# Moving matmul operands to other places modulo 512 bytes in a hybrid RWKV-7 / attention / gated-MLP layer

## The chip, the cores and the metric

The kernel runs on one core of one Trainium2 chip. The metric is the device time of one execution in microseconds (us), as a median over runs.

## The reference

One layer of a streaming encoder, 256 tokens by 2048 features, all in float32:

```python
u   = rms_norm(h) * g;  z = u @ w_in                 # 2048 -> 3360 + 1088 + 4096 columns
A   = rwkv7_mixer(z[:, :3360])                       # 16 heads x 64, a delta-rule scan
B   = mla_mixer(z[:, 3360:4448])                     # 8 heads, low-rank q and kv
g_rw, g_mla = split(sigmoid(z[:, 4448:]))
mix = (g_rw * (A @ w_branch_rw) + g_mla * (B @ w_branch_mla)) @ w_out
h  += rms_norm(mix)
up  = causal_dwconv(rms_norm(h) @ w_up)              # 2048 -> 2 x 5632, width 3
gate, val = split(up)
h  += rms_norm((gelu(gate) * val) @ w_down)          # 5632 -> 2048
h  += rms_norm(sigmoid(h @ w_ple_gate) * (p @ w_ple))
```

## The kernel before

Every large product is done in fp32r with both operands split into two parts, `hi` (the value rounded to fp32r) and `lo` (what is left), and three products of parts are summed: hi·hi, hi·lo and lo·hi. Weights come in chunks of 512 KB (128 partitions x 1024 numbers) on SyncE's DMA queue into one of three `raw` buffers; `wchunk` (L147 to L175) has ScalarE copy each half to a `hi` buffer (L166) and VectorE subtract it to a `lo` buffer (L167), five buffers of 128x512 of each kind.

Four helpers issue the matmuls. In the first two the weights are the stationary operand (128 columns, loaded anew for each matmul) and the activations move.

- `fm3` (L197): three matmuls of 256 columns for each weight block, hi·hi (L201), hi·lo (L202), lo·hi (L203). It serves the input projection (moving tile `uT`), the two branch projections (`ymla`, `yrw`) and the low-rank up-projections (`latm`).
- `fm` (L183): two matmuls for each weight block, one of 512 columns with the hi weights over the activation's hi and lo part in one go (L192, or L190 for the last block of a sum) and one of 256 columns with the lo weights over the hi part (L193, or L189). It serves the MLP's up-projection alone (tile `u2`, which the trace shows as `u`). The two halves of the PSUM bank are added later by `conv_sum`.
- `tm` (L208): here the activations are stationary (128 tokens) and the weights move, 512 columns: L214, L216, L218. It serves the products with `w_out` (stationary tile `mixs`), `w_down` (`fsplit`), `w_ple_gate` (`h2T`), and the value projection (`latm` stationary, moving `hi` and `lo`).
- small fp32 matmuls of the attention and of the RWKV scan are woven between the `fm3` matmuls.

An activation tile such as `uT` or `u2` holds 16 blocks of 512 numbers a partition, each block the 256 hi parts and then the 256 lo parts of 128 features. `fsplit` holds the two parts of one block of `f`, the MLP's middle activations, and stands in the pool `fs` at the right end of the memory.

Where a tile stands in a partition's memory is decided when the program is built. The buffers of the weights, `hi` and `lo`, all stand at 64 bytes modulo 512, and so does every 128-column block of them, which is 512 bytes long. The places of the other operand, in bytes modulo 512, in the built program:

| tile | role | before | after |
|---|---|---|---|
| `uT`, `ymla`, `yrw` | moving, 256 columns | 64 | 96 |
| `latm` | moving, 256 columns | 96 | 96 |
| `u2`, hi and lo in one | moving, 512 columns | 64 | lo part 64; hi part 96 (blocks 0 to 7), 64 (blocks 8 to 15) |
| `u2`, hi | moving, 256 columns | 64 | 96 (blocks 0 to 7), 64 (blocks 8 to 15) |
| `fsplit` | stationary | 480 | 64 |
| `mixs`, `h2T` | stationary | 64 | 64 |
| `latm` | stationary | 96 | 96 |

Of the kernel before, what the change touches and what calls it, by code (L numbers as in the profile page):

```python
# [7 lines left out]
F32 = mybir.dt.float32  # L8
F32R = mybir.dt.float32r
I32 = mybir.dt.int32  # L10
AF = mybir.ActivationFunctionType
ALU = mybir.AluOpType
# [3 lines left out]
P = 128  # L16
T = 256
D = 2048
KB = D // P
C = 64  # L20
NCH = T // C
NPAIR = 8
NFF = 44
WC = 1024
NH = 8
# [101 lines left out]
def hybrid_block(tc, A):  # L127
    nc = tc.nc
    es = ExitStack()
    mm = nc.tensor.matmul  # L130
    act = nc.scalar.activation
    tt = nc.vector.tensor_tensor
    ts = nc.vector.tensor_scalar
    stt = nc.vector.scalar_tensor_tensor
# [43 lines left out]
    def split(hi, lo, src):  # L178
        act(hi, src, AF.Copy)  # L179
        tt(out=lo, in0=src, in1=hi.bitcast(F32), op=ALU.subtract)  # L180


    def fm(ps, hi, lo, cols, mov, first, last):  # L183
        n = len(mov)
        for c, col in enumerate(cols):
            for i in range(n):
                f, l = first and i == 0, last and i == n - 1
                if l:
                    mm(ps[:, c, 0:T], lo(i, col, P), mov[i][:, 0:T], start=False, stop=False)  # L189
                    mm(ps[:, c, :], hi(i, col, P), mov[i], start=f, stop=True)  # L190
                else:
                    mm(ps[:, c, :], hi(i, col, P), mov[i], start=f, stop=False)  # L192
                    mm(ps[:, c, 0:T], lo(i, col, P), mov[i][:, 0:T], start=False, stop=False)  # L193


    def fm3(ps, hi, lo, cols, mov, first, last):
# [52 lines left out]
    def to_fm(ptile, dst, rows, gain, kbs):  # L249
        for k in range(kbs[0], kbs[1], 2):  # L250
            ps = ptile("tr")
            for kb in (k, k + 1):
                o = ps[:, (kb - k) * T:(kb - k) * T + T]
                for t in range(2):
                    nc.tensor.transpose(o[:, t * P:t * P + P], rows[:, t, kb * P:kb * P + P], ident)  # L255
                if gain is not None:
                    g = V(gain, kb)
                    a = act(dst[:, kb, 0:T], o, AF.Copy, scale=g)
                    v = stt(out=dst[:, kb, T:2 * T], in0=o, scalar=g, in1=dst[:, kb, 0:T].bitcast(F32),
                            op0=ALU.mult, op1=ALU.subtract)  # L260
            if gain is None:
                o = ps[:].rearrange("p (k t) -> p k t", k=2)
                a = act(dst[:, k:k + 2, 0:T], o, AF.Copy)
                v = tt(out=dst[:, k:k + 2, T:2 * T], in0=o, in1=dst[:, k:k + 2, 0:T].bitcast(F32), op=ALU.subtract)
        return a, v


# [1 line left out]
    esp = ExitStack()  # L269
    big = es.enter_context(tc.tile_pool(name="big", bufs=1))  # L270

    def act_tile(nm):
        return big.tile([P, KB, 2 * T], F32R, name=nm, tag="act")

    def row_tile(nm, s, shape=None, dt=F32):
        return big.tile(shape or [P, 2, D], dt, name=nm, tag=f"row{s}")

    uT = act_tile("uT")
    psd = esp.enter_context(tc.tile_pool(name="psd", bufs=4, space=PSUM))
    pss = esp.enter_context(tc.tile_pool(name="pss", bufs=2, space=PSUM))  # L280
    nsm = [0]
# [8 lines left out]
    xT = row_tile("xT", 0, [P, KB, T])  # L290
# [3 lines left out]

    def x_split(kb):
        g = V("g_pre", kb)
        act(uT[:, kb, 0:T], xT[:, kb, :], AF.Copy, scale=g)
        stt(out=uT[:, kb, T:2 * T], in0=xT[:, kb, :], scalar=g, in1=uT[:, kb, 0:T].bitcast(F32),
            op0=ALU.mult, op1=ALU.subtract)

    def x_part(q):
# [10 lines left out]
        nc.sync.dma_start(x, xr[:, t, c])  # L312
        act(x, x, AF.Square, accum_out=st[:, i:i + 1])

    umov = [uT[:, kb, :] for kb in range(KB)]
    es_z = ExitStack()
    zp = es_z.enter_context(tc.tile_pool(name="zp", bufs=2, side="right"))
    es_e = ExitStack()
# [112 lines left out]
    h, l = [], []  # L431
    for c in range(2):
        x_split(2 * c)
        hi = wp.tile([P, 512], F32R, name="hi", bufs=5)
        lo = wp.tile([P, 512], F32R, name="lo", bufs=5)
# [81 lines left out]
    ps = run(dense(umov, [A["w_in1"][q] for q in range(2)], 8, cols=(0,)))  # L517
# [7 lines left out]
    ps = run(win_duo(0))  # L525
# [24 lines left out]
    p = slice(64, 96)  # L550
# [7 lines left out]
    for i in range(2):  # L558
        p = slice(64 * i, 64 * i + 64)
# [11 lines left out]
    def u_part(q):  # L571

        for kb in range(4 * q, 4 * q + 4):
            stt(out=xT[:, kb, :], in0=xT[:, kb, :], scalar=V("g_pre", kb), in1=rsb[:], op0=ALU.mult, op1=ALU.mult)
        for kb in range(4 * q, 4 * q + 4, 2):
            split(uT[:, kb:kb + 2, 0:T], uT[:, kb:kb + 2, T:2 * T], xT[:, kb:kb + 2, :])

    qp = []
    for j in range(2):
        o = run(up2(A["w_q"][4 + j], cq))  # L580
# [20 lines left out]
    SC = float(192.0 ** -0.5)  # L601

    mix = row_tile("mix", 0, [P, KB, T])
    ymla = row_tile("ymla", 1, [P, NH, 2 * T], F32R)

    def attention(h, q, k):
        pr = []
# [64 lines left out]
        evac(mix[:, 2 * j:2 * j + 2, :], pb[:], scale=0.5)  # L672


    yrw = row_tile("yrw", 1, [P, NPAIR, 2 * T], F32R)
    es_e.close()
    es_e = ExitStack()
    ep = es_e.enter_context(tc.tile_pool(name="ep", bufs=1))
# [473 lines left out]
    xr2 = A["x"].rearrange("(t p) d -> p t d", p=P)  # L1152
    late_x = [load(h[:, t, c:c + 1024], xr2[:, t, c:c + 1024]) for t in range(2) for c in range(0, D, 1024)]
    mg = row_tile("mg", 1)
    u2 = act_tile("u2")
    with tc.tile_pool(name="gb", bufs=1) as gb, tc.tile_pool(name="pso", bufs=1, space=PSUM, reuse_waits="tile") as pso:
        gbc, gl = gain_bc(gb, A["g_pm"])
        tm_all(pso, A["w_out"], lambda kb: mixs[:, kb, :], post(gb, mg, gbc, 8), side=SIDE0 + gl + late_x)
# [6 lines left out]
    fp = es_f.enter_context(tc.tile_pool(name="fp", bufs=1))  # L1165
    f = fp.tile([P, NFF, T], F32, name="f")
    es_g = ExitStack()
    fsp = es_g.enter_context(tc.tile_pool(name="fs", bufs=4, side="right"))
    gb = es_g.enter_context(tc.tile_pool(name="gb2", bufs=1, side="right"))
    with tc.tile_pool(name="fw", bufs=2) as fw, tc.tile_pool(name="psu", bufs=3, space=PSUM, reuse_waits="tile") as psu:  # L1170
        u2m = [u2[:, kb, :] for kb in range(KB)]
        zc = [fp.tile([P, 2, T + 2], F32, name=f"zc{i}") for i in range(2)]
        for z in zc:
            nc.gpsimd.memset(z[:, :, 0:2], 0.0)

        def conv_sum(j, ps):
            z = zc[j % 2]
            y = fw.tile([P, 2, T], F32, name="cy")
            with tc.high_priority():
                act(y[:], ps[:, :, 0:T], AF.Copy)  # L1180
                tt(out=z[:, :, 2:T + 2], in0=ps[:, :, T:2 * T], in1=y[:], op=ALU.add)

        def conv(j):
            z = zc[j % 2]
            y = fw.tile([P, 2, T], F32, name="cy")
            tt(out=z[:, :, 2:T + 2], in0=z[:, :, 2:T + 2], in1=u2s[:].unsqueeze(1).to_broadcast([P, 2, T]), op=ALU.mult)  # L1186
            for c in range(2):
                m = j + NFF * c
                act(y[:, c, :], z[:, c, 2:T + 2], AF.Identity, bias=V("cb", m), scale=V("cw2", m))  # L1189
                stt(out=y[:, c, :], in0=z[:, c, 1:T + 1], scalar=V("cw1", m), in1=y[:, c, :], op0=ALU.mult, op1=ALU.add)  # L1190
                stt(out=y[:, c, :], in0=z[:, c, 0:T], scalar=V("cw0", m), in1=y[:, c, :], op0=ALU.mult, op1=ALU.add)  # L1191
            act(y[:, 0, :], y[:, 0, :], AF.Gelu_apprx_tanh)
            tt(out=f[:, j, :], in0=y[:, 0, :], in1=y[:, 1, :], op=ALU.mult)


        pu = {}
        for n, (j, q) in enumerate([(j, q) for q in range(4) for j in range(3)] + [(j, q) for j in range(3, NFF) for q in range(4)]):
            if q == 0:
                pu[j] = psu.tile([P, 2, 512], F32, name="d")
            ps = pu[j]  # L1200
            with queued(rows[n] if n < 2 else None):
                hi, lo = wchunk(A["w_up"][j, q], 4)
            fm(ps, hi, lo, [0, P], u2m[4 * q:4 * q + 4], q == 0, q == 3)
            if j < 2 and q == 3:
                conv_sum(j, ps)
            if (j, q) == (0, 3):
                with queued(rows[2]):
                    for t in range(2):
                        for g in range(4):
                            junk = gb.tile([P, 512], F32, name="junk", bufs=2)  # L1210
                            act(junk[:], h[:, t, g * 512:g * 512 + 512], AF.Square, accum_out=col4(18)[:, t, g:g + 1])
                r = st[:, 26:28]
                rstd4(r, 18)
            if (j, q) == (3, 0):

                rbr = fp.tile([P, 2, P], F32, name="rbr")
                for t in range(2):
                    act(rbr[:, t, :], r[:, t:t + 1].to_broadcast([P, P]), AF.Copy)
                prb = trp.tile([P, 512], F32, name="tr")
                for t in range(2):  # L1220
                    nc.tensor.transpose(prb[:, t * P:t * P + P], rbr[:, t, :], ident)
                u2s = fp.tile([P, T], F32, name="u2s")
                act(u2s[:], prb[:, 0:T], AF.Copy)
                conv(0)
                conv(1)
                conv_sum(2, pu[2])
                conv(2)
            if j > 2 and q == 3:
                conv_sum(j, ps)
                conv(j)  # L1230
# [4 lines left out]
    with tc.tile_pool(name="psw", bufs=1, space=PSUM, reuse_waits="tile") as psw:  # L1235
# [34 lines left out]
        def finish(t):  # L1270
# [3 lines left out]
            for a, n, q in ((0, 1024, nc.sync), (1024, 640, nc.scalar), (1664, 384, nc.sync)):  # L1274
# [6 lines left out]
        lp = es_f.enter_context(tc.tile_pool(name="late", bufs=1, reuse_waits="tile"))  # L1281
        late = lp.tile([P, 10, 2, 512], F32R, name="late")
        eg = lp.tile([P, 512], F32, name="eg")
        tm_all(psw, A["w_pg"], lambda kb: h2[:, kb, :], gated, 10, lambda i: (late[:, i, 0, :], late[:, i, 1, :]),
               after=rows)
    es_f.close()
    es_g.close()
# [100 lines left out]
```

## Time and profile before

| | |
|---|---|
| median of 3 runs | 1617.18 us (1614.29 to 1618.39) |
| the profiled execution | 1614.37 us, span 1612.6 us |
| PE busy | 1586.2 us, 98% of the span, 10624 matmuls |
| VectorE, ScalarE busy | 1191.5 us (74%), 968.6 us (60%) |
| DMA | 285.59 MB, 177 GB/s in the mean |
| granted TensorE clock | 1.00 of full speed (2.4 GHz) in all but the last stretch |

The span is the profiled execution from its first to its last instruction. Matmuls overlap in the pipeline, so the length of one (283 ns for 256 columns) is not what it costs: what counts is the distance from its start to the start of the next one. The stages in order of time: the input projection with attention and RWKV scan woven in (to 615 us), the RWKV branch (615 to 661), `w_out` (662 to 749), the MLP's up-projection (757 to 1257), `w_down` (1257 to 1503), the gate of the layer's embedding (1510 to 1600).

### The profile page before, as it was taken

To read this page: it belongs to the slowest core of one execution; us is meant where nothing else is said; L and a number is where in the kernel's file an instruction comes from. 1 tells how busy PE (TensorE), PEld (TensorE's weight loads), DVE (VectorE), ACT (ScalarE), POOL (GpSimd) and SP (SyncE) were. 2 spreads that over 40 slices of the span, in tenths; PEclk is the share of its full clock that TensorE was granted. 3 is DMA by queue.
4 is the path that set the end of the run, shared out by engine and by line. 5 is a ranking of instruction groups with operands and counts; after the bars stand their busy time and mean duration, and the time that the engine had idled before them with its cause. 6 is when DMAs were issued, how large, how long until landed. Compare 5 with 4: busy or idle time off the path is not lost.

```text
span 1612.6 us, 29281 instructions
## 1 busy us (share of the span) xinstructions
PE 1586.2 (98%) x10624; PEld 1420.6 (88%) x10624; DVE 1191.5 (74%) x2666; ACT 968.6 (60%) x2030; POOL 29.7 (2%) x78
## 2 busy tenths in 40 slices
PE   8999999999999999999999999999999999999997
PEld 8989999999999999887888888888888888888885
DVE  6796797878989566557787777777777655777866
ACT  6676656566565655456765555655555555666653
POOL 0000100000000001100000000000000000000000
PEclk9999999999999999999999999999999999999999
DMA  8654554444545455776566666666666666666564
GB/s 291 189 156 144 158 160 129 131 146 119 158 124 157 126 186 185 264 222 172 179 186 187 189 186 184 187 188 186 185 187 189 183 187 192 192 188 186 168 197 142
DMA packets 80048, 285.59 MB, mean 177 GB/s; under 512 B 8992, under 2 KB 10144, under 8 KB 79904
## 3 DMA queue, kind: packets, MB, share of 16 engines
q1 hardware_dynamic: 77616, 280.19, 57.3%
q10 hardware_dynamic: 2288, 3.55, 0.7%
q8 instruction: 83, 1.36, 0.3%
q14 instruction: 61, 0.50, 0.1%
HBM read 281.60 MB, written 2.10 MB: 176 GB/s over the span
## 4 chain that ended last, share of the span: by engine, by line
PE 57%; DVE 1%; ACT 0%; issue 0%; DVEq 0%; ACTq 0%
PE d L192 19%; PE d L193 10%; PE o L214 6%; PE o L216 6%; PE o L218 6%; PE e L216 2%; PE e L214 2%; PE e L218 2%; PE d L190 1%; PE d L189 1%; PE tr L255 0%; DVE h L1276 0%; DVE lo L167 0%; DVE h L1131 0%; ACT junk L1262 0%
## 5 line engine op out<-in xcount | busy, mean ns | idle before, releaser
L167 DVE TENSOR_TENSOR lo<-raw,hi 128x512 fp32r<-128x512 f32 x1012 | 685.9, 689 | 336.9 <-ACT hi L166 329.2
L166 ACT CAST hi<-raw 128x512 fp32r<-128x512 f32 x1012 | 612.6, 617 | 480.8 <-PE d L192 182.7
L192 PE MATMUL d<-u,hi 128*128 128x512 f32 x1320 | 470.8, 399 | 0.0
L193 PE MATMUL d<-u,lo 128*128 128x256 f32 x1320 | 371.3, 281 | 0.0
L201 PE MATMUL d<-uT,hi 128*128 128x256 f32 x1072 | 311.9, 291 | 5.1 <-ACT hi L179 5.1
L203 PE MATMUL d<-uT,lo 128*128 128x256 f32 x1072 | 305.5, 285 | 2.4 <-DVE lo L167 2.4
L202 PE MATMUL d<-uT,hi 128*128 128x256 f32 x1072 | 304.5, 284 | 0.0
L192 PEld LDWEIGHTS d<-u,hi 128*128 128x128 f32 x1320 | 248.1, 188 | 56.1
L193 PEld LDWEIGHTS d<-u,lo 128*128 128x128 f32 x1320 | 249.4, 189 | 4.3
L201 PEld LDWEIGHTS d<-uT,hi 128*128 128x128 f32 x1072 | 206.4, 193 | 6.9 <-ACT hi L179 5.1
L203 PEld LDWEIGHTS d<-uT,lo 128*128 128x128 f32 x1072 | 206.2, 192 | 3.4 <-DVE lo L167 2.9
L202 PEld LDWEIGHTS d<-uT,hi 128*128 128x128 f32 x1072 | 206.6, 193 | 0.1
L214 PE MATMUL o<-hi,fsplit 128*128 128x512 f32 x264 | 90.2, 396 | 0.0
L216 PE MATMUL o<-lo,fsplit 128*128 128x512 f32 x264 | 90.1, 395 | 0.0
L218 PE MATMUL o<-hi,fsplit 128*128 128x512 f32 x264 | 89.9, 394 | 0.0
L214 PEld LDWEIGHTS o<-hi,fsplit 128*128 128x128 f32 x264 | 49.6, 188 | 12.4
L216 PEld LDWEIGHTS o<-lo,fsplit 128*128 128x128 f32 x264 | 49.6, 188 | 12.0
L218 PEld LDWEIGHTS o<-hi,fsplit 128*128 128x128 f32 x264 | 49.6, 188 | 11.6
L180 DVE TENSOR_TENSOR fsplit<-f,fsplit 128x256 fp32r<-128x256 f32 x132 | 54.8, 419 | 0.0
L179 ACT ACTIVATE fsplit<-f 128x256 fp32r<-128x256 f32 x132 | 54.4, 413 | 0.7 <-ACT fsplit L179 0.5
L1189 ACT ACTIVATE cy<-zc,vec 128x256 f32<-128x256 f32 x88 | 52.7, 601 | 2.7 <-DVE zc L1186 2.6
L1191 DVE SCALAR_TENSOR_TENSOR cy<-zc,vec,cy 128x256 f32<-128x256 f32 x88 | 42.4, 482 | 1.5
(393 smaller groups left out, 2378.9 us busy)
## 6 DMA issues: line engine op xcount, KB each, us to landing
raw<-in_w_up SPq DMA_DIRECT2D x176, 512.0 KB, 3.6
raw<-in_w_in SPq DMA_DIRECT2D x133, 512.0 KB, 3.6
raw<-in_w_down SPq DMA_DIRECT2D x88, 512.0 KB, 4.3
raw<-in_w_out SPq DMA_DIRECT2D x32, 512.0 KB, 4.4
raw<-in_w_pg SPq DMA_DIRECT2D x32, 512.0 KB, 3.7
raw<-in_w_bm SPq DMA_DIRECT2D x16, 512.0 KB, 3.6
raw<-in_w_br SPq DMA_DIRECT2D x16, 512.0 KB, 4.2
raw<-in_w_kv SPq DMA_DIRECT2D x8, 512.0 KB, 3.6
```

Of the source, the lines that this page charges most:

```text
L166: nc.scalar.copy(hi[:], raw[:, c:c + 512])
L167: tt(out=lo[:], in0=raw[:, c:c + 512], in1=hi[:].bitcast(F32), op=ALU.subtract)
L179: act(hi, src, AF.Copy)
L180: tt(out=lo, in0=src, in1=hi.bitcast(F32), op=ALU.subtract)
L192: mm(ps[:, c, :], hi(i, col, P), mov[i], start=f, stop=False)
L193: mm(ps[:, c, 0:T], lo(i, col, P), mov[i][:, 0:T], start=False, stop=False)
L201: mm(ps[:, c, :], hi(i, col, P), mov[i][:, 0:T], start=f, stop=False)
L202: mm(ps[:, c, :], hi(i, col, P), mov[i][:, T:2 * T], start=False, stop=False)
L203: mm(ps[:, c, :], lo(i, col, P), mov[i][:, 0:T], start=False, stop=l)
L214: mm(b[:], h, hi(i, g * 512, 512), start=f, stop=False)
L216: mm(b[:], h, lo(i, g * 512, 512), start=False, stop=False)
L218: mm(b[:], x, hi(i, g * 512, 512), start=False, stop=l)
```

## The change

All tiles keep their sizes in numbers that are used, and every engine issues the same instructions in the same order with the same waits on the same semaphores; only addresses, and the access patterns of `fm`, differ.

- `uT` starts 8 numbers (32 bytes) into its allocation; `ymla` and `yrw` likewise.
- `u2` is laid out apart: first the 16 lo parts, then the 16 hi parts, the first eight of these 32 bytes further on, the last eight 512 bytes further on.
- `fm`'s 512-column matmul reads the lo part and then the hi part, through an access pattern of two runs of 256; so the lo-weight product is added to the second half of the PSUM bank and no longer to the first.
- A tile `pad` of 104 numbers (416 bytes) at the right end moves the pool `fs`, so that `fsplit` comes to 64 modulo 512.
- The allocations of `uT`/`u2`/`h2T` and of `ymla`/`yrw` grow by 128 numbers (512 bytes), which moves all that stands behind them by a multiple of 512 bytes.

```diff
@@ fm
+            o = ps[:, c, :].rearrange("p (a t) -> p a t", a=2)
             for i in range(n):
                 f, l = first and i == 0, last and i == n - 1
+                h, _, both = mov[i]
                 if l:
-                    mm(ps[:, c, 0:T], lo(i, col, P), mov[i][:, 0:T], start=False, stop=False)
-                    mm(ps[:, c, :], hi(i, col, P), mov[i], start=f, stop=True)
+                    mm(ps[:, c, T:2 * T], lo(i, col, P), h, start=False, stop=False)
+                    mm(o, hi(i, col, P), both, start=f, stop=True)
                 else:
-                    mm(ps[:, c, :], hi(i, col, P), mov[i], start=f, stop=False)
-                    mm(ps[:, c, 0:T], lo(i, col, P), mov[i][:, 0:T], start=False, stop=False)
+                    mm(o, hi(i, col, P), both, start=f, stop=False)
+                    mm(ps[:, c, T:2 * T], lo(i, col, P), h, start=False, stop=False)
@@ tiles
-    def act_tile(nm):
-        return big.tile([P, KB, 2 * T], F32R, name=nm, tag="act")
+    def act_tile(nm, o=lambda k: 0, apart=False):
+        t = big.tile([P, KB * 2 * T + 128], F32R, name=nm, tag="act")
+        if not apart:
+            return [(t[:, x:x + T], t[:, x + T:x + 2 * T], t[:, x:x + 2 * T]) for x in (o(k) + 2 * T * k for k in range(KB))]
+        return [(t[:, x:x + T], t[:, T * k:T * k + T],
+                 bass.AP(t[:].tensor, t[:, T * k:T * k + T].offset, [t[:].ap[0], [x - T * k, 2], [1, T]]))
+                for k, x in ((k, o(k) + KB * T + T * k) for k in range(KB))]
...
+    def y_tile(nm):
+        return row_tile(nm, 1, [P, 16 * T + 128], F32R)[:, 8:8 + 16 * T].rearrange("p (b t) -> p b t", b=8)
+
-    uT = act_tile("uT")
+    uT = act_tile("uT", lambda k: 8)
-    ymla = row_tile("ymla", 1, [P, NH, 2 * T], F32R)
+    ymla = y_tile("ymla")
-    yrw = row_tile("yrw", 1, [P, NPAIR, 2 * T], F32R)
+    yrw = y_tile("yrw")
-    u2 = act_tile("u2")
+    u2 = act_tile("u2", lambda k: 8 if k < 8 else 128, True)
@@ the pools of the MLP
     es_g = ExitStack()
+    es_g.enter_context(tc.tile_pool(name="pad", bufs=1, side="right")).tile([P, 104], F32, name="pad")
     fsp = es_g.enter_context(tc.tile_pool(name="fs", bufs=4, side="right"))
```

## Rows read from the trace of the kernel before

**Rows 1.** The page: span, busy time of each engine.

```profile
span 1612.6 us, 29281 instructions
PE 1586.2 (98%) x10624; PEld 1420.6 (88%) x10624; DVE 1191.5 (74%) x2666; ACT 968.6 (60%) x2030; POOL 29.7 (2%) x78
```

**Rows 2.** Busy time by stretch: densest for VectorE, and up-projection; clock, DMA, GB/s last.

```profile
360.00:460.00 100.00, 97.64 (x967) 95.29 (x966) 87.09 (x274) 62.73 (x165) 3.87 (x14) 1.00 0.45 136
860.00:1240.00 380.00, 380.00 (x2153) 329.59 (x2152) 286.88 (x505) 221.76 (x404) 0.00 (x0) 1.00 0.62 186
```

**Rows 3.** Longest waits of ScalarE and PE: total us, times, longest.

```profile
ACT hi L166 <- PE d L192: 182.7, 165, 1.5
...
PE d L201 <- ACT hi L179: 5.1, 1, 5.1
```

**Rows 4.** Matmuls by tile: ns least, median, most; first and last start in us.

```profile
L201 PE MATMUL d<-uT,hi x1072: 276/283/582, 5.1 to 614.5; 128*128 128x256 f32 x179
...
L201 PE MATMUL d<-yrw,hi x128: 283/283/284, 614.8 to 660.5; 128*128 128x256 f32 x128
...
L214 PE MATMUL o<-hi,fsplit x264: 394/394/400, 1257.4 to 1503.1; 128*128 128x512 f32 x132
...
L214 PE MATMUL e<-hi,fsplit x88: 392/394/395, 1380.6 to 1441.5; 128*128 128x512 f32 x88
...
L192 PE MATMUL d<-u,hi x1320: 390/398/482, 756.9 to 1256.6; 128*128 128x512 f32 x189
...
L190 PE MATMUL d<-u,hi x88: 395/400/400, 786.4 to 1257.1; 128*128 128x512 f32 x88
```

**Rows 5.** Timeline of PE in the input projection: start, length, instruction.

```profile
560.93 0.36 PE L201 MATMUL d<-uT,hi 128*128 128x256 f32 x1
561.13 0.28 PE L202 MATMUL d<-uT,hi 128*128 128x256 f32 x1
...
590.10 0.28 PE L201 MATMUL d<-uT,hi 128*128 128x256 f32 x1
...
592.98 0.28 PE L201 MATMUL d<-uT,hi 128*128 128x256 f32 x1
```

**Rows 6.** Timeline of PE in the RWKV branch projection.

```profile
619.85 0.28 PE L201 MATMUL d<-yrw,hi 128*128 128x256 f32 x1
...
622.73 0.28 PE L201 MATMUL d<-yrw,hi 128*128 128x256 f32 x1
```

**Rows 7.** Timeline of PE in the low-rank up-projections.

```profile
126.11 0.28 PE L201 MATMUL d<-latm,hi 128*128 128x256 f32 x1
...
128.56 0.28 PE L201 MATMUL d<-latm,hi 128*128 128x256 f32 x1
```

**Rows 8.** Timeline of PE in the product with `w_out`, stationary `mixs`.

```profile
679.68 0.62 PE L214 MATMUL o<-hi,mixs 128*128 128x512 f32 x2
...
683.76 0.62 PE L214 MATMUL o<-hi,mixs 128*128 128x512 f32 x2
```

**Rows 9.** Timeline of PE in the product with `w_down`, stationary `fsplit`.

```profile
1300.30 0.63 PE L218 MATMUL o<-hi,fsplit 128*128 128x512 f32 x2
...
1303.10 0.63 PE L218 MATMUL o<-hi,fsplit 128*128 128x512 f32 x2
```

**Rows 10.** Timeline of PE in the value projection, stationary `latm`.

```profile
94.13 0.40 PE L214 MATMUL dv<-hi,latm 128*128 128x512 f32 x1
...
96.93 0.40 PE L214 MATMUL dv<-hi,latm 128*128 128x512 f32 x1
```

**Rows 11.** Timeline of PE in the MLP's up-projection.

```profile
1000.13 0.40 PE L192 MATMUL d<-u,hi 128*128 128x512 f32 x1
1000.37 0.28 PE L193 MATMUL d<-u,lo 128*128 128x256 f32 x1
1000.49 0.40 PE L192 MATMUL d<-u,hi 128*128 128x512 f32 x1
...
1001.19 0.40 PE L192 MATMUL d<-u,hi 128*128 128x512 f32 x1
```

More of the change, by code (lines that the diff above doesn't have):

```diff
@@ L257, in to_fm @@
                     g = V(gain, kb)
-                    a = act(dst[:, kb, 0:T], o, AF.Copy, scale=g)
-                    v = stt(out=dst[:, kb, T:2 * T], in0=o, scalar=g, in1=dst[:, kb, 0:T].bitcast(F32),
+                    a = act(dst[kb][0], o, AF.Copy, scale=g)
+                    v = stt(out=dst[kb][1], in0=o, scalar=g, in1=dst[kb][0].bitcast(F32),
                             op0=ALU.mult, op1=ALU.subtract)
@@ L262, in to_fm @@
                 o = ps[:].rearrange("p (k t) -> p k t", k=2)
-                a = act(dst[:, k:k + 2, 0:T], o, AF.Copy)
-                v = tt(out=dst[:, k:k + 2, T:2 * T], in0=o, in1=dst[:, k:k + 2, 0:T].bitcast(F32), op=ALU.subtract)
+                hi, lo = (two(dst[k][x], dst[k + 1][x]) for x in range(2))
+                a = act(hi, o, AF.Copy)
+                v = tt(out=lo, in0=o, in1=hi.bitcast(F32), op=ALU.subtract)
         return a, v
@@ L270, in hybrid_block, with two @@
     big = es.enter_context(tc.tile_pool(name="big", bufs=1))
-    def act_tile(nm):
-        return big.tile([P, KB, 2 * T], F32R, name=nm, tag="act")
+    def act_tile(nm, o=lambda k: 0, apart=False):
[5 more added lines that the diff above has]
+                for k, x in ((k, o(k) + KB * T + T * k) for k in range(KB))]
+    def two(a, b):
+        return bass.AP(a.tensor, a.offset, [a.ap[0], [b.offset - a.offset, 2], a.ap[1]])
     def row_tile(nm, s, shape=None, dt=F32):
         return big.tile(shape or [P, 2, D], dt, name=nm, tag=f"row{s}")
-    uT = act_tile("uT")
+    def y_tile(nm):
+        return row_tile(nm, 1, [P, 16 * T + 128], F32R)[:, 8:8 + 16 * T].rearrange("p (b t) -> p b t", b=8)
+    uT = act_tile("uT", lambda k: 8)
     psd = esp.enter_context(tc.tile_pool(name="psd", bufs=4, space=PSUM))
@@ L296, in x_split @@
         g = V("g_pre", kb)
-        act(uT[:, kb, 0:T], xT[:, kb, :], AF.Copy, scale=g)
-        stt(out=uT[:, kb, T:2 * T], in0=xT[:, kb, :], scalar=g, in1=uT[:, kb, 0:T].bitcast(F32),
+        act(uT[kb][0], xT[:, kb, :], AF.Copy, scale=g)
+        stt(out=uT[kb][1], in0=xT[:, kb, :], scalar=g, in1=uT[kb][0].bitcast(F32),
             op0=ALU.mult, op1=ALU.subtract)
@@ L313, in stat_part @@
         act(x, x, AF.Square, accum_out=st[:, i:i + 1])
-    umov = [uT[:, kb, :] for kb in range(KB)]
+    umov = [b[2] for b in uT]
     es_z = ExitStack()
@@ L575, in u_part @@
         for kb in range(4 * q, 4 * q + 4, 2):
-            split(uT[:, kb:kb + 2, 0:T], uT[:, kb:kb + 2, T:2 * T], xT[:, kb:kb + 2, :])
+            split(*(two(uT[kb][x], uT[kb + 1][x]) for x in range(2)), xT[:, kb:kb + 2, :])
     qp = []
@@ L1170, in hybrid_block @@
     with tc.tile_pool(name="fw", bufs=2) as fw, tc.tile_pool(name="psu", bufs=3, space=PSUM, reuse_waits="tile") as psu:
-        u2m = [u2[:, kb, :] for kb in range(KB)]
+        u2m = u2
         zc = [fp.tile([P, 2, T + 2], F32, name=f"zc{i}") for i in range(2)]
@@ L1283, in hybrid_block @@
         eg = lp.tile([P, 512], F32, name="eg")
-        tm_all(psw, A["w_pg"], lambda kb: h2[:, kb, :], gated, 10, lambda i: (late[:, i, 0, :], late[:, i, 1, :]),
+        tm_all(psw, A["w_pg"], lambda kb: h2[kb][2], gated, 10, lambda i: (late[:, i, 0, :], late[:, i, 1, :]),
                after=rows)
```

## The prediction, on record before the changed kernel ran

> **What bounds the kernel now.** I first read the page: PE is busy for 1586.2 of 1612.6 us, VectorE for 74% and ScalarE for 60% [rows 1]. An average could hide a stage with another limit, so I next read stretches. In the up-projection PE is busy for all of 380 us; in the stretch where VectorE is densest, 360 to 460 us, VectorE stands at 87.09 of 100 us and PE still at 97.64 [rows 2]. The waits say who sets the pace: ScalarE's longest wait is that for the up-projection's matmuls to give a `hi` buffer back, 182.7 us in 165 waits, while PE's longest single wait is one of 5.1 us at the start [rows 3]. So the weights are made ahead of need, and what PE saves per matmul shortens the kernel, as long as it saves a few per cent.
>
> PE's busy share says nothing of how fast it goes. For that I read the timeline and took distances from start to start, because matmuls overlap. The same shape has two prices:
>
> - 256 columns moving, place 64, weights at 64: with `uT` 24 matmuls take 592.98 − 590.10 = 2.88 us, 120.0 ns each [rows 5]; with `yrw` 24 take 622.73 − 619.85 = 2.88 us, the same [rows 6].
> - 256 columns moving, place 96, weights at 64: with `latm` 21 matmuls of the same helper take 128.56 − 126.11 = 2.45 us, 116.7 ns each [rows 7].
> - 512 columns moving at 64, stationary at 64: with `mixs` 18 matmuls take 683.76 − 679.68 = 4.08 us, 226.7 ns each [rows 8].
> - 512 columns moving at 64, stationary elsewhere: with `fsplit` (480) 12 take 1303.10 − 1300.30 = 2.80 us [rows 9], with `latm` (96) 12 take 96.93 − 94.13 = 2.80 us [rows 10]; 233.3 ns each.
>
> The helper, the columns, the instruction mix and the clock (1.00, its 2.4 GHz level [rows 2]) are the same within each pair; the place modulo 512 bytes is what differs. A weight block is read while the matmul before it streams, so two reads of the same memory run side by side, and I take it that they delay each other by their relative place. Equal places are the better ones for 512 columns and the worse ones for 256.
>
> The Trainium skill speaks against this. "TensorE: Matmul & The Clock Gate", Part 2, "Step-by-step: what each phase is for", says that PE has two independent read ports and that "Loading the next tile's weights doesn't steal SBUF read bandwidth from the running matmul". By that rule no place should cost anything and the sum below would be 0. The trace does not agree: 116.7 against 120.0 and 226.7 against 233.3 ns at one clock.
>
> **The change part by part.** No instruction, wait or order changes, so every term is a count of matmuls times a difference of distances. VectorE and ScalarE write as many numbers to the new places as before, and I cost that at nothing; what covers it is that they wait for PE [rows 3].
>
> *`uT` to place 96.* 3 × 1072 = 3216 matmuls [rows 4] go from the price of rows 5 to that of rows 7: 3.33 ns each, 10.7 us if all gain. Those next to one of the scan's small matmuls stand at other distances (561.13 − 560.93 = 0.20 us [rows 5]) that need not shrink; I take six in seven, 9.2 us. Bounds: 0 and 10.7.
>
> *`ymla` and `yrw` to place 96.* Each 3 × 128 = 384 matmuls (the count is shown for `yrw` [rows 4]). `yrw` stands alone on PE: 384 × 3.33 ns = 1.3 us. `ymla` is woven like `uT`: 1.1 us. Together 2.4 us.
>
> *`fsplit` to place 64.* 3 × (264 + 88) = 1056 matmuls [rows 4] go from the price of rows 9 to that of rows 8, 6.67 ns each: 7.0 us. Nothing else is woven in here. This is the safest term.
>
> *`u2` apart, half of it 32 bytes off.* 1320 + 88 = 1408 pairs of a 512- and a 256-column matmul [rows 4]. Three pairs take 1001.19 − 1000.13 = 1.06 us, 353.3 ns a pair [rows 11]. No row has a moving operand of two runs with two places, so I bound it. The best that nearby rows allow is 226.7 + 116.7 = 343.4 ns [rows 7, 8]: 9.9 ns less a pair, 14 us for all. The worst is the longest distances seen in this stage on every pair, 0.24 + 0.12 us [rows 11]: 6.7 ns more, 9.4 us lost. The value I take: in blocks 0 to 7 (704 pairs) the 256-column matmul is that of rows 7, hi part at 96 and weights at 64, and gains 3.33 ns, 2.3 us; the 512-column one starts on the lo part at 64 as before, and the weights read beside it are 128 columns alone, so its second half matters little: 0. In blocks 8 to 15 all places modulo 512 are as before: 0.
>
> *What is given back.* Where VectorE is at 87% [rows 2], PE's next dense stretch will now and then reach a scan step or a weight half that isn't ready. I take 1 us. What would be late next there is VectorE's `lo` and the scan's results; over the whole weave that cover gone would cost at most the `uT` and `ymla` terms, 10.3 us.
>
> Sum: 9.2 + 2.4 + 7.0 + 2.3 − 1.0 = 19.9 us. The profiled execution took 1614.37 us, so 1594.5 us; it lies 2.8 us under the median of the runs shown, 1617.18, which by the same sum goes to 1597.3. I forecast 1595.
>
> **The rivals.**
>
> *The up-projection gains in full.* If the distances there come from the same clash as elsewhere, and breaking the row of equal places frees both matmuls of a pair, all 1408 pairs reach 343.4 ns: 14 in place of 2.3 us, 1583 us. For it: a pair costs 353.3 ns, 10 more than the two best prices added. Against it: half of the blocks keep their places.
>
> *The up-projection loses.* The 512-column matmul reads two runs, of which the second stands elsewhere, and settles at the long distances of rows 11: 9.4 us lost in place of 2.3 gained, 1607 us. For it: 512 columns like equal places best [rows 8 to 10], and in blocks 0 to 7 half of the columns leave theirs.
>
> *Nothing changes.* Place is not the cause, or the scan's chain sets the weave and takes the gain back. For it: the skill's rule above, by which it would be 1614 to 1617 us. Against it: five tiles in five stages fall into the two prices by place alone, and PE hardly waits [rows 3].
>
> *Slower.* The pattern of two runs costs the 512-column matmul a restart between the runs. No row shows such a restart; the nearest is the distance after a foreign matmul, 0.20 against 0.12 us [rows 5], so between 0 and 80 ns each. It decides at (18.6 gained elsewhere, less the 1.0 given back, + 4.9) / 1408 = 16 ns: above that the kernel is slower by over 0.3%; at 80 ns it would lose 113 us and end at 1709. Against it: the prices that place makes in these rows are 3 to 7 ns a matmul, and a restart of 16 ns or more would be of another kind; but it is the step of which the trace shows least.
>
> **How the numbers follow.** My forecast (1590 to 1600 us) has 0.50; the up-projection in full (1580 to 1590) 0.22; the up-projection losing (1600 to 1608) 0.13; nothing changes 0.08; slower 0.07. About 0.3%, 4.9 us, is what a measurement of this kernel can tell from no change. Faster by more: the first three and a part of the fourth's upper edge, 0.86. Within: 0.07. Slower: 0.07. The range that leaves out nothing changed and slower, and a little of the outer ends of the second and third, is 1581 to 1607; it holds the bounds of `u2` on both sides (1583 and 1607).
>
> **What would show it.** In the trace after: 24 `uT` matmuls in 2.80 us where there were 2.88; `yrw` the same; 12 `fsplit` matmuls in 2.72 in place of 2.80 us; three `u2` pairs of blocks 0 to 7 in 1.05 us and of blocks 8 to 15 in 1.06; the up-projection's length, 757 to 1257 us before, shorter by 2 to 3 us and `w_down`'s by 7; ScalarE still waiting for PE. I am wrong if `uT` or `fsplit` keep their distances, if the 512-column distances of `u2` leave 0.23 to 0.24, or if PE's waits in the weave grow by more than some us.

## The result, and the profile after

The changed kernel takes 1601.12 us in the median of 4 runs (1598.50 to 1601.52), the kernel before, run beside it, 1617.79 us. The ratio is 0.9897 with a 95% interval of 0.9883 to 0.9911: 16.7 us less, where the forecast of 1595 us meant 22. The profiled execution took 1598.50 us against 1614.37, 15.9 us less, where its sum said 19.9.

The page after: span, PE's busy time, and ScalarE's copies with what ended the idle time before them.

```profile
span 1596.7 us, 29281 instructions
PE 1567.3 (98%) x10624; PEld 1409.5 (88%) x10624; DVE 1191.9 (75%) x2666; ACT 968.7 (61%) x2030; POOL 29.7 (2%) x78
...
L166 ACT CAST hi<-raw 128x512 fp32r<-128x512 f32 x1012 | 612.5, 617 | 464.6 <-PE d L194 180.0
```

PE's share is the same 98% as in [rows 1], and ScalarE still waits for PE's matmuls: the kernel has the same bound, and PE goes through its matmuls faster. Matmuls by tile after, first and last start at the end of each row:

```profile
L203 PE MATMUL d<-latm,hi x80: 276/280/468, 77.2 to 149.5; 128*128 128x256 f32 x80
...
L203 PE MATMUL d<-yrw,hi x128: 277/279/280, 610.4 to 654.9; 128*128 128x256 f32 x128
...
L194 PE MATMUL d<-u,hi x1320: 387/395/480, 751.3 to 1247.8; 128*128 128x512 f32 x189
...
L216 PE MATMUL o<-hi,fsplit x264: 389/389/397, 1248.5 to 1487.2; 128*128 128x512 f32 x132
```

Against [rows 4] the stage starts give the account. `yrw` starts at 610.4 in place of 614.8 us (4.4 gained before it), lasts to the last start 44.5 in place of 45.7 us (1.2 to 1.3), `u` runs from 751.3 to 1247.8 in place of 756.9 to 1256.6 (496.5 for 499.7: 3.2 gained), and `fsplit`'s first to last start is 238.7 in place of 245.7 (7.0). 4.4 + 1.3 + 3.2 + 7.0 = 15.9 us, which is the whole difference of the spans. Of the 4.4 us, 1.7 are there before the first `latm` matmul (77.2 in place of 78.9 us); that start moves between executions of any of these kernels (below), so these 1.7 us are luck.

The timeline of PE after, six pieces of it:

```profile
323.14 0.28 PE L204 MATMUL d<-uT,hi 128*128 128x256 f32 x1
323.58 0.39 PE L205 MATMUL d<-uT,lo 128*128 128x256 f32 x1 [0.16 <-DVE lo L167]
...
585.75 0.28 PE L203 MATMUL d<-uT,hi 128*128 128x256 f32 x1
...
588.55 0.28 PE L203 MATMUL d<-uT,hi 128*128 128x256 f32 x1
...
614.99 0.28 PE L203 MATMUL d<-yrw,hi 128*128 128x256 f32 x1
...
617.79 0.28 PE L203 MATMUL d<-yrw,hi 128*128 128x256 f32 x1
...
994.93 0.39 PE L194 MATMUL d<-u,hi 128*128 128x512 f32 x1
...
995.98 0.40 PE L194 MATMUL d<-u,hi 128*128 128x512 f32 x1
...
997.39 0.40 PE L194 MATMUL d<-u,hi 128*128 128x512 f32 x1
...
998.45 0.40 PE L194 MATMUL d<-u,hi 128*128 128x512 f32 x1
...
1290.21 0.62 PE L220 MATMUL o<-hi,fsplit 128*128 128x512 f32 x2
...
1292.93 0.62 PE L220 MATMUL o<-hi,fsplit 128*128 128x512 f32 x2
```

24 `uT` matmuls in 2.80 us and 24 `yrw` in 2.80 us (2.88 in [rows 5, 6]); 12 `fsplit` in 2.72 (2.80 in [rows 9]); three `u2` pairs of blocks 0 to 7 in 1.05 us (from 994.93) and three of blocks 8 to 15 in 1.06 (from 997.39; [rows 11]). These are the distances that the forecast named. The first piece is what it did not name: the third matmul of a group comes 0.44 us after the second, where 0.12 is the rule, because VectorE's `lo` half of the weights is late. The row puts only 0.16 us of that down as idle, since the matmul before it counts as busy for its whole 0.28 us.

### The profile page after: what moved, and what is told of

It is laid out like the page before. It is cut to its first block, busy times and chain, and to the rows that moved or that the text cites. A ratio compares the mean times of both kernels' runs of the same rounds, so it can differ in the third digit from the quotient of the medians.

```text
span 1596.7 us, 29281 instructions
## 1 busy us (share of the span) xinstructions
PE 1567.3 (98%) x10624; PEld 1409.5 (88%) x10624; DVE 1191.9 (75%) x2666; ACT 968.7 (61%) x2030; POOL 29.7 (2%) x78
## 4 chain that ended last, share of the span: by engine, by line
PE 91%; DVE 4%; ACT 2%; DMA 1%; issue 1%; POOL 0%; ACTq 0%; DVEq 0%; POOLq 0%
PE d L194 19%; PE d L195 10%; PE d L203 9%; PE d L205 9%; PE d L204 9%; PE o L216 6%; PE o L218 6%; PE o L220 6%; PE e L216 2%; PE e L218 2%; PE e L220 2%; PE d L192 1%; DVE lo L167 1%; PE d L191 1%; PE px L866 1%
## 5 line engine op out<-in xcount | busy, mean ns | idle before, releaser
L203 PE MATMUL d<-uT,hi 128*128 128x256 f32 x1072 | 308.4, 288 | 5.7 <-ACT hi L179 5.1
L205 PE MATMUL d<-uT,lo 128*128 128x256 f32 x1072 | 302.0, 282 | 3.1 <-DVE lo L167 3.1
L204 PE MATMUL d<-uT,hi 128*128 128x256 f32 x1072 | 300.8, 281 | 0.0
L203 PEld LDWEIGHTS d<-uT,hi 128*128 128x128 f32 x1072 | 202.9, 189 | 7.8 <-ACT hi L179 5.1
L205 PEld LDWEIGHTS d<-uT,lo 128*128 128x128 f32 x1072 | 202.6, 189 | 5.0 <-DVE lo L167 4.3
L204 PEld LDWEIGHTS d<-uT,hi 128*128 128x128 f32 x1072 | 202.9, 189 | 0.1
L220 PE MATMUL o<-hi,fsplit 128*128 128x512 f32 x264 | 88.4, 389 | 0.0
L216 PE MATMUL o<-hi,fsplit 128*128 128x512 f32 x264 | 88.4, 389 | 0.0
```

What stands on the lines that cost most here:

```text
L203: mm(ps[:, c, :], hi(i, col, P), mov[i][:, 0:T], start=f, stop=False)
L204: mm(ps[:, c, :], hi(i, col, P), mov[i][:, T:2 * T], start=False, stop=False)
L205: mm(ps[:, c, :], lo(i, col, P), mov[i][:, 0:T], start=False, stop=l)
L216: mm(b[:], h, hi(i, g * 512, 512), start=f, stop=False)
L220: mm(b[:], x, hi(i, g * 512, 512), start=False, stop=l)
```

## The experiments

Two theories stood against each other on each of two questions. First, is it the relative place modulo 512 bytes that sets the distance, or something else that differs between the tiles? Second, why did the input projection with the weave give back more than half of its gain: because VectorE has too much to do, or because of the scan's own order of steps?

**The moving tiles of `fm3` put back.** Only `fsplit` and `u2` stay changed.

```diff
-    uT = act_tile("uT", lambda k: 8)
+    uT = act_tile("uT")
...
-        return row_tile(nm, 1, [P, 16 * T + 128], F32R)[:, 8:8 + 16 * T].rearrange("p (b t) -> p b t", b=8)
+        return row_tile(nm, 1, [P, 16 * T + 128], F32R)[:, 0:16 * T].rearrange("p (b t) -> p b t", b=8)
```

> The changed kernel with uT, ymla and yrw back at the weights' place, so that only fsplit and u2 stay changed. Theory (the terms add, and the gain of uT and ymla in the weave is mostly taken back by late weight halves and scan steps): 1606.8 us, that is the changed kernel plus 4.4 us before 615 us and plus 1.3 us in the RWKV branch. Rival (the uT term came through in full and something else lost time): 1612 us.

Measured: 1606.28 us in the median of 5 (1605.77 to 1607.28), ratio to before 0.9940 (0.9927 to 0.9954). That is near the expected 1606.8: the terms add, and the `fm3` tiles together are worth 1606.28 − 1601.12 = 5.2 us (7.0 by the two ratios, each to runs of the kernel before beside it), not the 11.6 of my terms. In its trace `latm` and `yrw` stand so, and below them `latm` in the kernel before:

```profile
L203 PE MATMUL d<-latm,hi x80: 276/280/468, 81.3 to 153.7; 128*128 128x256 f32 x80
...
L203 PE MATMUL d<-yrw,hi x128: 283/283/283, 617.8 to 663.5; 128*128 128x256 f32 x128
```

```profile
L201 PE MATMUL d<-latm,hi x80: 276/280/468, 78.9 to 151.2; 128*128 128x256 f32 x80
```

`yrw` starts 7.4 us later than in the changed kernel, but `latm` already 4.1 us later: the first `latm` matmul comes anywhere from 77.2 to 81.3 us in the traces of this case, with old places and with new. From the first `latm` to the first `yrw` matmul it is 536.5 us here, 533.2 in the changed kernel, and 535.9 (614.8 − 78.9) in the kernel before. That stretch, "the weave" below, is the sounder measure: the change gains 2.7 to 3.3 us in it. It has an uncertainty of its own: three kernels below with the same weave as the changed kernel take 532.3, 533.5 and 534.0 us, so the gain is 2 to 4 us.

**Places swept.** Two kernels give each block of `uT` and of `h2T` another place, so that one trace shows many; a third changes `u2` alone.

```diff
-    uT = act_tile("uT", lambda k: 8)
+    uT = act_tile("uT", lambda k: 8 * k)
...
-            o = ps[:, c, :].rearrange("p (a t) -> p a t", a=2)
+            o = ps[:, c, :]
...
-    u2 = act_tile("u2", lambda k: 8 if k < 8 else 128, True)
+    u2 = act_tile("u2", lambda k: (8, 16, 64, 120)[k // 4])
...
-    h2 = act_tile("h2T")
+    h2 = act_tile("h2T", lambda k: 8 * k)
```

> The changed kernel with uT's block k at 32k bytes past the weights' place (0, 32, ... 480), u2 contiguous again (hi then lo) with each quarter of its blocks at 32, 64, 256 and 480 bytes past it, and h2T's stationary block k at 32k bytes past it. Read block by block in the trace. Theory (relative place modulo 512 sets the distance): uT block 0 at 120.0 ns, block 1 at 116.7 ns, the others on a few levels between 113 and 122 by block; h2T block 0 at 226.7, block 1 at 233.3, block 13 (416) at 233.3, others between 226 and 240. Rival A (place is not the cause): all blocks of a tile at one distance. Rival B (only whether the place is an odd or even multiple of 32 bytes counts): blocks alternate 120.0 and 116.7, and 226.7 and 233.3.

The second, with `uT` and `h2T` at `lambda k: k` and `u2` apart, its hi parts at `(8, 16, 64, 120)[k // 4]`:

> The changed kernel with uT's block k at 4k bytes past the weights' place (0 to 60), u2 apart with the lo parts at the weights' place and the hi parts of each quarter of the blocks at 32, 64, 256 and 480 bytes past it, and h2T's stationary block k at 4k bytes past it. Theory (relative place sets the distance): block 0 of uT at 120.0 and block 8 (32 bytes) at 116.7 ns; block 0 of h2T at 226.7 and block 8 at 233.3; where it turns in between is not known. u2's first quarter at 349 ns a pair as in the changed kernel. Rival (place is not the cause): all blocks of a tile at one distance.

The third, with the lo parts of `u2` at `(8, 16, 64, 120)[k // 4]` and the hi parts at a multiple of 512 bytes:

> The changed kernel with u2's hi parts all at the weights' place and the lo parts of each quarter of the blocks at 32, 64, 256 and 480 bytes past it; nothing else differs. If in the changed kernel the hi part's place beside the weights is what saved 4 ns a pair in blocks 0 to 7, the pairs here stay at 352 to 353 ns in all quarters (up-projection 500 us). If it is that the two runs of one matmul have different places, some quarter falls to 349 ns or less.

A fourth and a fifth tried more places by quarters of the blocks. In the fourth the offsets fall at some borders of quarters, so that parts of `u2` overlap there by up to 104 numbers:

> The changed kernel with the quarters of uT's blocks at 16, 192, 448 and 480 bytes past the weights' place, and u2 apart with the quarters' lo and hi parts at (288, 32), (448, 0), (32, 256) and (0, 448). Theory (a chunk of 24 matmuls at one place settles to that place's distance): uT's quarters at 114 to 118 ns, the third the lowest (115.6 in the sweep by block); u2's second quarter near 346.7 ns a pair as with 480, the fourth near 348.6, no quarter above 353. Rival (the sweep by block read the passage from one place to the next, not the places): uT's quarters all at 116.7.

> The changed kernel with u2 contiguous (hi then lo, fm's patterns as before the change) and the quarters of its blocks at 16, 192, 288 and 448 bytes past the weights' place. Theory (each place has its distance): 346 to 351 ns a pair by quarter; 448 and 16, lowest for 256 columns, may be lowest here too, 343 to 346. Rival (any unequal place does the same): 347 in all quarters, as with 32.

Measured, as mean distance in ns from a matmul's start to the next, over matmuls followed by one at the same place, long waits left out; place is bytes past the weights' place (for `h2T`: the moving weights stay, the stationary block moves):

| `uT`, 256 columns | ns | | `h2T`, 512 columns | ns |
|---|---|---|---|---|
| 0 (whole tile, kernel before) | 119.8 | | 0 (whole tile) | 227.0 |
| 32 (whole tile, changed kernel) | 117.0 | | 32 | 233.2 |
| 448 (a quarter) | 115.7 | | 448 | 229.6 |
| 16, 192 (quarters) | 116.5, 116.6 | | 256 | 227.8 |
| 480 (a quarter) | 118.1 | | 192 | 229.9 |
| 96, 352 (one block) | 119.3 | | the other multiples of 32 | 232 to 234 |
| 4, 52 (one block) | 122.1, 122.0 | | 4 to 60 in steps of 4 | 230.6 to 235.1 |

| `u2`, first run and second run | ns a pair | | | ns a pair |
|---|---|---|---|---|
| hi 0, lo 0 in one (before) | 352.8 | | lo 0, hi 32 (changed, blocks 0 to 7) | 349.0 |
| 16 in one | 346.7 | | lo 0, hi 0 (changed, blocks 8 to 15) | 352.0 |
| 32 in one | 347.1 | | lo 0, hi 64; 480; 448 | 348.6; 348.6; 348.8 |
| 256; 288 in one | 347.5; 348.8 | | lo 0, hi 256 | 353.1 |
| 448; 480 in one | 349.9; 350.3 | | lo 256; 480, hi 0 | 346.6; 346.7 |
| 64; 192 in one | 350.6; 351.1 | | lo 32; 64; 448, hi 0 | 349.3; 351.2; 350.9 |
| | | | lo 288, hi 32; lo 32, hi 256 | 348.3; 350.8 |

That place is the cause is shown: one tile in one stage goes through the whole set of prices as its blocks move, and the rival of one distance for all falls. Not told apart is the place relative to the weights from the moved tile's own place, because the weights stood at 64 in every run. The rival of odd and even multiples of 32 bytes falls too: of the even ones, 0 costs 119.8 and 448 only 115.7. A block beside blocks at other places reads up to 3 ns off its settled value, so the single-block rows are rough: in the first sweep `uT` at 0 and at 32 reads 118.7 and 118.2, where 120.0 and 116.7 were expected and 119.8 and 117.0 are the settled values. For 512 columns against a stationary block the equal place is the best as a whole tile, but its single block reads 229.9 in the first sweep, above 256 with 227.8, so the order of these two is open. For the pairs the trace shows no simple rule. Two expectations on them missed: with the lo part at 448 and the hi part at 0 a pair costs 350.9 ns, where 346.7 was expected, and neither 16 nor 448 in one came to 343 to 346.

The third kernel had the lowest time of these five, 1595.62 us in its one run. Its up-projection shows 2.7 us of that, with 493.8 us from first to last start in place of 496.5 in the changed kernel:

```profile
L194 PE MATMUL d<-u,hi x1320: 387/392/481, 751.0 to 1244.8; 128*128 128x512 f32 x189
```

The guess in its expectation that only the hi part's place matters falls: with all hi parts at the weights' place two of the quarters cost 346.6 and 346.7 ns.

**`u2` whole, 32 bytes off.** The two runs of the change given up; `fm` reads hi and lo in one go as before.

```diff
-            o = ps[:, c, :].rearrange("p (a t) -> p a t", a=2)
+            o = ps[:, c, :]
...
-    u2 = act_tile("u2", lambda k: 8 if k < 8 else 128, True)
+    u2 = act_tile("u2", lambda k: 8)
```

> The changed kernel with u2 again contiguous, hi then lo, and all of it 32 bytes past the weights' place; fm's patterns as before the change. Theory (the lower price per pair seen in the first quarter of the sweep, 347.1 ns, holds for all blocks): up-projection 492 us in place of 497, whole kernel about 5 us less than the changed kernel, 1596 us. Rival (the low price belongs to blocks beside others at other places): pairs at 349 to 352 ns and no gain.

Measured: 1595.57 us in the median of 4 (1593.57 to 1599.51), ratio to before 0.9879 (0.9858 to 0.9900). The interval overlaps that of the changed kernel; the stage itself is clearer. Its timeline and its tile:

```profile
994.77 0.39 PE L194 MATMUL d<-u,hi 128*128 128x512 f32 x1
...
999.63 0.39 PE L194 MATMUL d<-u,hi 128*128 128x512 f32 x1
```

```profile
L194 PE MATMUL d<-u,hi x1320: 390/390/484, 753.6 to 1245.5; 128*128 128x512 f32 x189
```

14 pairs in 4.86 us, 347.1 ns each, and 491.9 us from first to last start in place of 496.5. So the arrangement in two runs is not needed, and the plain shift by 32 bytes gains 4.6 us more than it.

**VectorE's work cut in the weave.** Both layouts of `uT`, `ymla` and `yrw`, with the scan's 16x16 solve left out.

```diff
-                for i in range(o, o + 3):
-                    nc.vector.stream_shuffle(out=rp16[:, i, :], in_=dg[:].rearrange("p r c j -> p (r c j)"),
...
-                tt(out=pd[:, :, 0:t + 1], in0=x8[:, :, 0:t + 1], in1=r8[:, :, 0:t + 1, t], op=ALU.mult)
-                nc.vector.tensor_reduce(out=x8[:, :, t], in_=pd[:, :, 0:t + 1], axis=AX.X, op=ALU.add)
```

> The changed kernel, and the scan's solve of the 16x16 blocks left out (shuffles, products and reductions, about 45 us of VectorE's work in the weave; the blocks' inverse is then taken as the identity). To be read beside the same cut with uT, ymla and yrw at the weights' place. Theory (VectorE, late with weight halves and scan steps, took the weave's gain back): the RWKV branch's first matmul comes 8 to 9 us earlier with the new places than with the old ones, where it is 4.4 us with the solve in. Rival (the scan's own order of dependent steps or the small matmuls take it back, whatever VectorE has to do): 4 to 5 us.

> As the run before, with uT, ymla and yrw at the weights' place. The base of that comparison: first matmul of the RWKV branch at 605 to 612 us by either theory.

The tiles of the first, with the new places, and then of the second, with the old ones:

```profile
L203 PE MATMUL d<-latm,hi x80: 276/280/468, 79.0 to 151.3; 128*128 128x256 f32 x80
...
L203 PE MATMUL d<-yrw,hi x128: 277/279/280, 608.6 to 653.1; 128*128 128x256 f32 x128
```

```profile
L203 PE MATMUL d<-latm,hi x80: 276/280/469, 79.0 to 151.4; 128*128 128x256 f32 x80
...
L203 PE MATMUL d<-yrw,hi x128: 283/283/284, 614.9 to 660.6; 128*128 128x256 f32 x128
```

The weave takes 529.6 us with the new places and 535.9 with the old: 6.3 us, against 2 to 4 with the solve in. That lies between the 8 to 9 us of the theory and the 4 to 5 of the rival, and both had the old layout's `yrw` at 605 to 612 us, where it came at 614.9. The 8 to 9 us were more than there is: from `latm` on, the short distances (under 127 ns for 256 columns, under 243 for 512) from one dense matmul (of `fm3` or `tm`, not a small one of the scan or the attention) to the next sum to 379.9 us in 3136 with the old places and 372.1 in 3137 with the new ones, 7.8 us less. The other side is as telling: at the old places the cut gains nothing or 0.6 us (535.9 and 536.5 with the solve, 535.9 without), at the new ones 3.6 us. So the weave was bound by PE before and is bound in part by VectorE's side after. The semaphores, which tell whose result ended a wait, agree. Beyond 118 ns for a matmul of 256 columns and 230 for one of 512, the long distances that ended with a result of VectorE make 6.5 us before and 8.6 in the changed kernel, and without the solve 5.2 and 5.5; those that ended with one of ScalarE grow with the solve (1.6 to 2.9 us) and without it (2.0 to 2.8). The cut takes away VectorE's work and, with it, steps that the scan waits for. So it does not tell VectorE's load from the scan's own order.

**More dense work for each step of the scan, and some of VectorE's work given away.** All three on top of `u2` whole at 32 bytes.

```diff
-STEP, SUB = 2.4, 1.56
+STEP, SUB = 2.47, 1.6
```

> u2 contiguous and 32 bytes past the weights' place, as in the run of that alone, and 2.47 and 1.6 in place of 2.4 and 1.56 units of dense work for each step of the scan, so that a step has as much time as before the change. Theory A (what takes the weave's gain back is that scan steps come too soon after each other for VectorE): from the first latm matmul to the first yrw matmul 531 us in place of 533.5, whole kernel 1593. Theory B (it is the weight halves, so VectorE's work as a whole): no change, 533 us and 1595.5.

> As the run before, with 2.6 and 1.69 units. Theory A: as that run or 1 us less still, until the dense work runs out before the scan ends, which would cost several us. Theory B: no change or slower.

```diff
-        tt(out=be[:], in0=kk[:], in1=a[:], op=ALU.mult)
+        nc.gpsimd.tensor_tensor(out=be[:], in0=kk[:], in1=a[:], op=ALU.mult)
...
-        ts(out=a[:], in0=a[:], scalar1=V("k_a", j), scalar2=oka[:, j:j + 1], op0=ALU.mult, op1=ALU.add)
+        act(a[:], a[:], AF.Identity, scale=V("k_a", j), bias=oka[:, j:j + 1])
...
-        tt(out=y[:], in0=y[:], in1=bc4(gs[:, 0, :]), op=ALU.subtract)
+        nc.gpsimd.tensor_tensor(out=y[:], in0=y[:], in1=bc4(gs[:, 0, :]), op=ALU.subtract)
...
-        tt(out=y[:], in0=y[:], in1=bc4(gs[:, 2, :]), op=ALU.mult)
+        nc.gpsimd.tensor_tensor(out=y[:], in0=y[:], in1=bc4(gs[:, 2, :]), op=ALU.mult)
...
-        stt(out=m, in0=g[:], scalar=1.0, in1=m, op0=ALU.add, op1=ALU.mult)
+        act(g[:], g[:], AF.Copy, bias=1.0)
+        nc.gpsimd.tensor_tensor(out=m, in0=g[:], in1=m, op=ALU.mult)
```

> u2 contiguous and 32 bytes past the weights' place, as in the run of that alone, and about 19 us of VectorE's work in the weave given to others: a scaling and the gate's addition to ScalarE, four products or differences of the scan and gate to GpSimd. Theory (VectorE's work as a whole takes the weave's gain back): from the first latm matmul to the first yrw matmul 531 to 532 us in place of 533.5, whole kernel 1593 to 1594. Rival (GpSimd's slower operations delay the scan, or hold VectorE up, by more than they free): 534 us or more, 1596 or more.

With 2.47 units the weave takes 532.5 in place of 533.5 us and the kernel 1595.76 us (ratio 0.9869, 0.9854 to 0.9884): no change that can be told from none (the same weave varies from 532.3 to 534.0), as theory B had it. With 2.6 it takes 535.1 us in the weave and 1603.04 us in all (0.9921, 0.9909 to 0.9934): worse, which both theories allowed. Most of that loss comes behind the weave: PE stands still for 2.9 us before the product with `w_out`, and the granted clock is then 0.63 from 663 to 669 us, so most of that stretch is at its 1.2 GHz level. Giving work away took 1604.01 us (0.9932, 0.9919 to 0.9946), 539.0 us in the weave: the rival's outcome. Its longest waits of PE after 79 us, and VectorE's `lo` halves between 150 and 580 us:

```profile
PE d L205 <- DVE lo L167: 4.1, 8, 1.6
```

```profile
L167 DVE TENSOR_TENSOR lo<-raw,hi 128x512 fp32r<-128x512 f32 x219 | 155.0, 713 | 63.2 <-ACT hi L166 61.5 <-PE d L205 1.0
```

Against it, the same row of the kernel without the relief:

```profile
L167 DVE TENSOR_TENSOR lo<-raw,hi 128x512 fp32r<-128x512 f32 x224 | 153.1, 687 | 60.6 <-ACT hi L166 58.9 <-PE d L205 1.0
```

The halves became slower, 713 for 687 ns, and later. The trace shows why they became slower: the 193 that no instruction of GpSimd overlaps took 686 ns in the mean and 697 at most, as before; the 26 that one overlaps took 913, eight of them 1.1 to 1.7 us. One of these, and the GpSimd instruction beside it:

```profile
509.68 1.71 DVE L167 TENSOR_TENSOR lo<-raw,hi 128x512 fp32r<-128x512 f32 x1
```

```profile
509.56 1.27 POOL L992 TENSOR_TENSOR mix<-g,mix 128x512 f32<-128x512 f32 x1 [12.82 <-ACT g L991]
```

So the work given to GpSimd stood in VectorE's way, and this run does not speak against the theory that VectorE's work takes the gain back. How much of the 5.5 us lost in the weave that makes, and how much the longer steps of the scan, was not told apart.

## Why the prediction was right, and where its sizes were off

That place sets the distances, the sign and the range held: 1601.1 us lies in 1581 to 1607, 6 us above the forecast of 1595. It lies outside the forecast's own band of 1590 to 1600 and in the one given to the losing up-projection (0.13), which is not what happened: the up-projection gained, and the time is missing in the weave. Of the sum's 19.9 us 15.9 came, 1.7 of them by the luck of an early `latm`.

- *Place sets the distance.* Right, and shown by putting tiles back and by sweeping blocks. The same matmuls differ by up to 6 ns for 256 and 8 ns for 512 columns by place alone. That loading the next tile's weights takes no read bandwidth from the running matmul ("TensorE: Matmul & The Clock Gate", Part 2, "Step-by-step: what each phase is for", in the Trainium skill) is thus not borne out: with `fsplit` only the place of the stationary operand changed, and the matmuls of 512 columns went from 233.3 to 226.7 ns.
- *`fsplit`.* 7.0 us forecast, 7.0 measured, the price of [rows 8] met to 0.1 ns.
- *`yrw`.* 1.3 forecast, 1.2 to 1.3 measured.
- *`uT` and `ymla`, and "What is given back".* Here two sizes were off. The two terms, 9.2 and 1.1 us, came to 7.4: in the weave alone the short distances shrank from 379.6 us in 3134 to 370.1 us in 3117, of which the 17 that became long, at 0.12 us each, are no gain. The price of 3.33 ns was read from two short pieces; over all short distances `uT` goes from 119.8 to 117.0 ns, 2.8 less. The term that I set at 1 us without a working, the late `lo` halves and scan steps, measured 4 to 5 us in the weave (7.4 less the 2.7 that came through): the long distances after a dense matmul, those to the scan's small matmuls among them, summed to 48.0 us in 226 before and to 54.0 us in 243 after. I took "PE hardly waits" from [rows 3], and the waits view shows about half of it: PE's idle time in the weave grows from 5.6 to 8.2 us, for a wait shorter than what is left of the matmul before it is no idle time. The long distances from start to start are where the whole stands. By the semaphores 2 us of the growth ended with VectorE's results and 1.3 with ScalarE's; for the rest no cause was found. Nor does the loss keep to the stretch where VectorE is at 87% [rows 2]: counted in lots of 400 dense matmuls, with about 1 us to be had in each, 0.7 us came through in each of the two from 146 to 270 us, and 0.2 to 0.4 us in each of the four from there to 536 us.
- *`u2`.* 2.3 us forecast, 3.2 measured. The sum was near by luck, the reasoning was not: the 512-column matmul's distance fell (236.0 to 231.4 ns in blocks 0 to 7) and the 256-column one's did not (116.8 to 117.6). The step that priced the second run at 0 failed; a pair has to be priced as a whole.
- *The rivals.* No restart between two runs shows: in blocks 8 to 15, where the runs have equal places, a pair costs 352.0 ns, against 352.8 before in one run. "In full" at 343.4 ns a pair was reached by no place tried; the lowest is 346.6.

The cut of the solve shows that VectorE's side holds the weave in part. Whether it is VectorE's work as a whole or the order of the scan's steps stays open, and so do a relief without new delays and the rule behind the prices of the pairs.

## What to carry to other kernels

Measure a stream of matmuls by the distance from start to start, tile by tile, beside the place of its two operands modulo 512 bytes; when one helper shows two prices, moving a tile by 32 bytes is nearly free to try, and a sweep of one tile's blocks gives a dozen places in one trace, roughly. When every matmul gets 2 to 3% faster, price what the next engine will be late with: here more than half of the weave's gain was lost, and PE's idle time showed half of that loss.

## What the runs showed of the hardware that was not expected

- Steps finer than 32 bytes matter: `uT` 4 bytes past the weights' place costs 122.1 ns, more than at the equal place (119.8), and 16 bytes past it 116.5.
- For 512 moving columns with the stationary block moved, the equal place (227.0 ns as a whole tile) and 256 bytes (227.8 in a sweep) are the cheapest; for 256 columns the equal place (119.8 ns) is among the dear ones.
- A `lo` half on VectorE (512 numbers a partition) took 686 ns in the mean where no GpSimd instruction overlapped it, and 913 where one did, up to 1712; not every overlap lengthens it.
